# Values of all heads of a branch in one unit with 512 columns moving, and fewer filler steps inside the attention

## The chip, the cores and the metric

One core of a Trainium2 chip runs the program once per measurement. The metric is device time in microseconds (us), lower is better. Engines: PE (matmul), DVE, ACT, POOL, SP; PEld is PE's weight load.

## What is computed

One transformer block on x (512 tokens, width 1024), float32. The reference, cut to what matters:

```python
h = h + 0.5 * swiglu(rmsnorm(h, ffn1_norm), ffn1_w_gu, ffn1_w_down)
u = rmsnorm(h, mix_norm)
qa, ka, va, qb, kb, vb, qi, ki, wi, g = jnp.split(u @ w_in, SPLIT_POINTS, axis=-1)
# 8 heads of 64 in each branch; q and k are normalised per head
out_a = dsa_attention(qa, ka, va, qi, ki, wi, bias_dsa)  # keys: the top 256 by an index score
out_b = moba_attention(qb, kb, vb, bias_moba)            # keys: blocks of 256
g_a, g_b = jnp.split(sigmoid(g + b_gate), 2, axis=-1)
mixed = g_a * (out_a @ w_branch_dsa) + g_b * (out_b @ w_branch_moba)
h = h + mixed @ w_out
h = h + 0.5 * swiglu(rmsnorm(h, ffn2_norm), ffn2_w_gu, ffn2_w_down)
```

## The kernel before, in words

Activations lie transposed: a tile holds 128 features by 512 tokens. Every float32 factor is split into a high part (rounded to the fast matmul format) and the rest, and a product takes three matmuls, hi x hi, hi x lo and lo x hi (`mm3`, lines 125 to 128). Weights come through `wunit` (L119): one DMA of 128x1024 on SP's queue, one ACT copy to the high part (L111), POOL subtractions for the low part (L117); three buffers each.

The stages: first feed-forward layer (`ffn`; its `lead1` begins with four PSUM banks in turn, two `mm` and two `s`, three matmuls each), then q, k, values and index scores, the attention of branch 1 (moba), the mix of branch 1, the attention of branch 0 (dsa), the mix, the output projection and the second feed-forward layer.

PE's order is the program's own. The other engines' instructions are put in an order by a scheduler, which the program steers with priorities and, for the search of the top keys, with a table: `PIN` names after which of the 32 logits of branch 1's attention the search for query tile 1, 2 or 3 may begin. `topk` (L532) runs 16 rounds of MAX8, MATCH_VALUE_LOAD and MATCH_REPLACE8 on DVE for each tile; its result is added to the logits of branch 0 (L578).

`attention` (L551) is a generator that walks 32 steps, i = 4 * head + query tile. At each it issues the logits of step i + 2 (L595, L596; DVE adds bias and finds the extremes at L604, ACT takes the exponential at L75), the transposes of step i (L636; ACT L646 and DVE L647 split the result), at every fourth the values product of the head before (L657, L658), and in branch 1 at every second an index score (`extra`). Between these it yields 1: `weave` then takes one step of the filler, a chain of other units. Before, there are three such steps per i. A filler step of a q, k or gate unit is one `mm3` with 512 columns; a unit has eight. `AHEAD_B` (12) and `AHEAD_A` (16) steps run ahead of the attention. What is left of the filler runs behind it.

A q unit's norm (L416) follows 4 steps after its post, a k unit's (L450, L451) 11 steps after (`later`, `tick`).

`v_units` (L467) makes the values of four heads of a branch for all tokens. There the activations are stationary and the weights move: 256 columns, four token tiles of eight k each, two tiles to a bank; a step is two `mm3`. The posts (L475 on ACT, L476 on DVE) write high and low parts. It runs four times: once before branch 1's attention (in the `s` banks), twice in that attention's filler and once in that of branch 0, in the three `mm` banks.

## Time and profile before

| what | value |
|---|---|
| median of 3 runs | 1142.54 us (1142.5 to 1144.0) |
| the profiled execution's own time | 1144.06 us |
| its span | 1142.3 us |
| mean granted clock of PE | 0.999 |
| busy: PE, DVE, ACT, POOL | 1133.5, 644.0, 468.9, 547.8 us |

The profile is of one execution; times in it count from the span's start. Busy time is the union of an engine's instructions. Matmuls overlap in the records, so their pace is read from the distance of their starts, not from their durations. A granted clock of 1.00 is the upper of two levels (2.4 GHz), 0.5 the lower (1.2 GHz).

### The profile page before, as it was taken

Reading aid. Unit: us, or ns where it says so; the run is one execution under the profiler, and the core shown is the slowest. Engines: PE = TensorE matmul, PEld = TensorE weight load, DVE = VectorE, ACT = ScalarE, POOL = GpSimd, SP = SyncE. Lnnn points to the kernel's source line nnn. Section 1 sums busy time; section 2 is a strip of 40 time slices with the busy share of each in tenths; the row PEclk is TensorE's granted clock in tenths of the full one; section 3 lists DMA queues with packets and bytes.
Section 4 is the critical chain, followed back from the end, with each engine's and each line's share of the span. In section 5 each row is a group of like instructions: output and inputs, shape, how many; then the busy total and the mean of one; then the engine's idle time right before and its main releaser. Section 6 shows DMA issues by size and latency. Waiting matters only on the chain.

```text
span 1142.3 us, 14230 instructions
## 1 busy us (share of the span) xinstructions
PE 1133.5 (99%) x5364; PEld 948.2 (83%) x5364; DVE 644.0 (56%) x966; ACT 468.9 (41%) x765; POOL 547.8 (48%) x438
## 2 busy tenths in 40 slices
PE   9999999999999999999999999999999999999998
PEld 7778888888888888888889888888888888888887
DVE  5864155622556358699958785754663156613651
ACT  6322122322235468767238765443332123312321
POOL 3444444444445674664565542174444444444442
PEclk9999999999999999999999999999999999999999
DMA  7233222322223222321332321422233232322222
GB/s 236 86 112 107 93 92 96 107 92 92 97 80 105 86 105 85 102 75 47 102 129 86 105 79 47 137 94 93 96 108 92 92 100 102 93 92 95 104 79 92
DMA packets 39580, 111.73 MB, mean 98 GB/s; under 512 B 4534, under 2 KB 9048, under 8 KB 39512
## 3 DMA queue, kind: packets, MB, share of 16 engines
q1 hardware_dynamic: 39368, 110.80, 29.4%
q8 instruction: 42, 0.69, 0.2%
q14 instruction: 26, 0.21, 0.1%
q10 hardware_dynamic: 144, 0.02, 0.0%
HBM read 108.64 MB, written 2.17 MB: 97 GB/s over the span
## 4 chain that ended last, share of the span: by engine, by line
PE 90%; DVE 5%; ACT 2%; issue 1%; POOL 1%; DMA 0%; SPq 0%; POOLq 0%; DVEq 0%; ACTq 0%
PE mm L126 21%; PE mm L127 21%; PE mm L128 21%; PE s L126 7%; PE s L128 7%; PE s L127 7%; PE pt L636 1%; DVE l L604 1%; PE s L595 1%; PE s L596 1%; PE o L658 1%; PE o L657 1%; POOL wlo L117 1%; ACT tmp L75 1%; DVE work L541 0%
## 5 line engine op out<-in xcount | busy, mean ns | idle before, releaser
L117 POOL TENSOR_TENSOR wlo<-raw,whi 128x256 fp32r<-128x256 f32 (+2 forms) x344 | 490.4, 1444 | 532.2 <-ACT whi L111 526.2
L111 ACT ACTIVATE whi<-raw 128x1024 fp32r<-128x1024 f32 (+2 forms) x207 | 205.2, 993 | 527.2 <-PE mm L127 345.7
L126 PE MATMUL mm<-x,whi 128*128 128x512 f32 x632 | 251.5, 398 | 1.4 <-DVE v L476 1.1
L128 PE MATMUL mm<-x,wlo 128*128 128x512 f32 x632 | 246.6, 390 | 0.0
L127 PE MATMUL mm<-x,whi 128*128 128x512 f32 x632 | 246.6, 390 | 0.0
L127 PE MATMUL mm<-a,whi 128*128 128x512 f32 (+1 forms) x462 | 178.7, 387 | 0.3
L126 PE MATMUL mm<-a,whi 128*128 128x512 f32 (+1 forms) x462 | 178.5, 386 | 0.0
L128 PE MATMUL mm<-a,wlo 128*128 128x512 f32 (+1 forms) x462 | 178.5, 386 | 0.0
L128 PEld LDWEIGHTS mm<-x,wlo 128*128 128x128 f32 x632 | 118.6, 188 | 25.7 <-DVE wlo L113 0.4
L126 PEld LDWEIGHTS mm<-x,whi 128*128 128x128 f32 x632 | 118.9, 188 | 24.1 <-DVE v L476 1.5
L126 PE MATMUL s<-x,whi 128*128 128x512 f32 x352 | 137.0, 389 | 0.6 <-ACT tmp L75 0.6
L127 PE MATMUL s<-x,whi 128*128 128x512 f32 x352 | 136.9, 389 | 0.0
L128 PE MATMUL s<-x,wlo 128*128 128x512 f32 x352 | 136.9, 389 | 0.0
L127 PEld LDWEIGHTS mm<-x,whi 128*128 128x128 f32 x632 | 119.0, 188 | 21.2 <-issue 0.5
L279 DVE SCALAR_TENSOR_TENSOR h<-mm,h 128x512 f32<-128x512 f32 (+1 forms) x49 | 33.4, 681 | 166.6 <-PE mm L128 166.6
L270 DVE TENSOR_TENSOR tmp<-tmp,tmp 128x512 f32<-128x512 f32 x44 | 99.0, 2249 | 29.3 <-ACT tmp L75 29.1
L154 DVE TENSOR_TENSOR a<-tmp,a 128x512 fp32r<-128x512 f32 x49 | 89.5, 1828 | 28.5 <-ACT a L153 28.3
L127 PEld LDWEIGHTS mm<-a,whi 128*128 128x128 f32 x462 | 86.8, 188 | 18.6 <-DVE a L154 1.1
L126 PEld LDWEIGHTS mm<-a,whi 128*128 128x128 f32 x462 | 86.8, 188 | 17.7
L128 PEld LDWEIGHTS mm<-a,wlo 128*128 128x128 f32 x462 | 86.8, 188 | 17.6
L126 PEld LDWEIGHTS s<-x,whi 128*128 128x128 f32 x352 | 66.0, 187 | 14.7 <-ACT tmp L75 1.0
L127 PEld LDWEIGHTS s<-x,whi 128*128 128x128 f32 x352 | 66.1, 188 | 13.8
(172 smaller groups left out, 1338.3 us busy)
## 6 DMA issues: line engine op xcount, KB each, us to landing
raw<-in_ffn_w_gu_dram SPq DMA_DIRECT2D x84, 512.0 KB, 3.5
raw<-in_w_in_dram SPq DMA_DIRECT2D x35, 512.0 KB, 3.5
raw<-in_ffn_w_down_dram SPq DMA_DIRECT2D x32, 512.0 KB, 3.5
raw<-in_ffn_w_down_dram SPq DMA_DIRECT2D x16, 384.0 KB, 3.1
bias<-fd SPq DMA_DIRECT2D x16, 256.0 KB, 3.4
raw<-in_w_v_dram SPq DMA_DIRECT2D x8, 512.0 KB, 3.4
raw<-in_w_out_dram SPq DMA_DIRECT2D x8, 512.0 KB, 3.5
h<-in_x_dram SPq DMA_DIRECT2D x8, 256.0 KB, 4.3
```

The lines of the kernel that those rows point to most:

```text
L75: op = after([group["load"]], lambda: nc.scalar.activation(*a, **k))
L111: nc.scalar.activation(hi, raw, AF.Copy)
L117: eng.tensor_sub(lo[:, b], raw[:, b], f32(hi)[:, b])
L126: nc.tensor.matmul(pt, wh, xh, start=start, stop=False)
L127: nc.tensor.matmul(pt, wh, xl, start=False, stop=False)
L128: nc.tensor.matmul(pt, wl, xh, start=False, stop=stop)
L154: nc.vector.tensor_sub(lo, src, f32(hi))
L270: nc.vector.tensor_mul(g1, g1, s)
L279: nc.vector.scalar_tensor_tensor(h[c][:, b], pd, 0.5, h[c][:, b], op0=ALU.mult, op1=ALU.add)
L595: nc.tensor.matmul(p[:, 0:N], qb, k[:, e, 0:N], start=True, stop=False)
L596: nc.tensor.matmul(p[:, 0:N], qb, kl[:, e, 0:N], start=False, stop=True)
L604: sums[i] = nc.vector.tensor_tensor_reduce(out=pe, in0=p[:, 0:W], in1=pe, scale=f[:, 2 * qt + e:2 * qt + e + 1], scalar=3e38, op0=ALU.add, ...
```

## The change

A value unit now makes all eight heads of a branch: weights move with 512 columns, one PSUM bank per token tile, four banks open at once, a step is one `mm3`, 32 steps to a unit. The values of pair 0 lie in a `g` buffer, those of pairs 1 to 3 in one `v` buffer. The unit of branch 1 runs wholly before its attention, that of branch 0 between the two attentions, in front of branch 1's mix. The attention of branch 1 takes two filler steps per i instead of three, that of branch 0 two and three in turn. All searches for top keys begin behind the last logits of branch 1. Gate 0 stands before the last pair's units of branch 0, and gates 3 to 6 lie in `g` and `q` buffers two by two. The columns of `w_v` are laid out anew on the host (eight units of 256 rows by 512 columns).

```diff
--- before.py
+++ after.py
@@ -30,7 +30,7 @@
 TMPS, RAWS = 7, 3
 AHEAD_A, AHEAD_B, GATES, GATES_B = 16, 12, 7, 3
 
-PIN, EVERY = (0, 20, 28, 31), 2
+PIN, EVERY = (0, 31, 31, 31), 2
 
 LAG, LAG_Q = 11, 4
 
@@ -464,38 +464,31 @@
 
         later(LAG, norm)
 
-    def v_units(br, j, dsts, bank=mmps):
-
-
-        vs = []
-
-        def post(t, p):
-            for e, v in enumerate(vs):
-                src = p[:, e * P:(e + 1) * P].rearrange("p (e d) -> p e d", e=2)
-                nc.scalar.activation(v[:, t, :, 0, :], src, AF.Copy, scale=r2T[:, t:t + 1])
-                nc.vector.scalar_tensor_tensor(v[:, t, :, 1, :], src, r2T[:, t:t + 1], f32(v)[:, t, :, 0, :],
-                                               op0=ALU.mult, op1=ALU.subtract)
-
-        ws = [wunit(w_v[4 * br + 2 * j + i]) for i in range(2)]
-        wh, wl = ([a.rearrange("p k c -> p (k c)").rearrange("p (k c) -> p k c", k=4)[:, k] for a in w for k in range(4)]
-                  for w in zip(*ws))
-        for t in range(NQ):
-            if t % 2 == 0:
-                p = bank()
-            o = p[:, (t % 2) * 256:(t % 2 + 1) * 256]
-            b = slice(t * P, (t + 1) * P)
-            for k in range(KD):
-                mm3(o, us[k][0][:, b], us[k][1][:, b], wh[k], wl[k], k == 0, k == KD - 1)
-                if k % 2:
+    def v_units(br, heads, banks):
+
+
+        va, vb = T("g", 1, (P, 2, S), F32R), T("v", 1, (P, 6, S), F32R)
+        va, vb = (a.rearrange("p n c -> p (n c)").rearrange("p (t e s d) -> p t e s d", t=NQ, s=2, d=DH)
+                  for a in (va, vb))
+        for j, dst in enumerate(heads):
+            v = va if j == 0 else vb[:, :, 2 * j - 2:2 * j]
+            dst.append(v.rearrange("p t e s d -> p t e (s d)"))
+        for m in range(4):
+            wh, wl = (a.rearrange("p k c -> p (k c)").rearrange("p (k c) -> p k c", k=2) for a in wunit(w_v[4 * br + m]))
+            for t, p in enumerate(banks):
+                b = slice(t * P, (t + 1) * P)
+                for i in range(2):
+                    k = 2 * m + i
+                    mm3(p, us[k][0][:, b], us[k][1][:, b], wh[:, i], wl[:, i], k == 0, k == KD - 1)
                     tick()
                     yield
-            if t == 1:
-                vs.extend(T("v", 3, (P, NQ, 2, 2, DH), F32R) for _ in dsts)
-                for v, dst in zip(vs, dsts):
-                    dst.append(v.rearrange("p t e s d -> p t e (s d)"))
-            if t % 2:
-                post(t - 1, p[:, 0:256])
-                post(t, o)
+        for t, p in enumerate(banks):
+            src = p.rearrange("p (e d) -> p e d", d=DH)
+            r = r2T[:, t:t + 1]
+            for v, c in ((va, src[:, 0:2]), (vb, src[:, 2:8])):
+                nc.scalar.activation(v[:, t, :, 0, :], c, AF.Copy, scale=r)
+                nc.vector.scalar_tensor_tensor(v[:, t, :, 1, :], c, r, f32(v)[:, t, :, 0, :],
+                                               op0=ALU.mult, op1=ALU.subtract)
 
     def qk_units(br, pr, q, k):
         u = (U_QA, U_QB)[br] + pr
@@ -682,7 +675,8 @@
                 values(i // 4 - 1)
             if extra and i % EVERY == 0:
                 extra.pop(0)()
-            yield 1
+            if sel and i % 2:
+                yield 1
         yield 3
         values(7)
 
@@ -703,12 +697,10 @@
     def gate(gi, keep):
 
         def post(p):
-            if gi in (3, 4):
-                g1 = T("g", 2)
-            elif gi in (5, 6):
-                if gi == 5:
-                    wide.append(T("q", 2, (P, 2, S)))
-                g1 = wide[0][:, gi - 5, :]
+            if 3 <= gi <= 6:
+                if gi % 2:
+                    wide.append(T("g", 1, (P, 2, S)) if gi == 3 else T("q", 2, (P, 2, S)))
+                g1 = wide[-1][:, 1 - gi % 2, :]
             else:
                 g1 = tmp()
             nc.vector.tensor_mul(g1, p, r2)
@@ -729,14 +721,15 @@
     def qk(br, pr):
         return qk_units(br, pr, *(dsa, moba)[br][pr][0:2])
 
-    def vv(br, j, **kw):
-        return v_units(br, j, [a[2] for a in (dsa, moba)[br][2 * j:2 * j + 2]], **kw)
+    def vv(br, banks):
+        return v_units(br, [a[2] for a in (dsa, moba)[br]], banks)
 
     piece[0] = 256
     ps3 = [mmps() for _ in range(2)]
     together([mmk(p, wunit(w_in[U_QB + 4 * i]), us) for i, p in enumerate(ps3)])
-    v0 = vv(1, 0, bank=sps)
-    next(v0)
+    v0 = vv(1, [sps(), sps(), T("o", 1, p=ps), mmps()])
+    for _ in range(2):
+        next(v0)
     r2 = norm_r(ss2)
     for _ in range(6):
         next(v0)
@@ -762,19 +755,19 @@
     ob, oa = [], []
     extra = [lambda qt=qt, hd=hd: score(qt, hd) for qt in range(1, NQ) for hd in range(4)]
     gates = {}
-    fill = chain(qk(1, 1) + qk(1, 2) + [vv(1, 1)] + qk(1, 3) + [gate(KD + c, gates) for c in range(GATES_B)]
-                 + qk(0, 0) + [vv(0, 0)])
+    fill = chain(qk(1, 1) + qk(1, 2) + qk(1, 3) + [gate(KD + c, gates) for c in range(GATES_B)] + qk(0, 0))
     weave(attention(1, moba, ob, extra), fill, AHEAD_B)
     run(fill)
     for qt in range(1, NQ):
         topk(qt)
+    run(vv(0, [sps(), sps(), T("o", 1, p=ps), tps()]))
     mixb = [T("a", 16) for _ in range(KD)]
     for c in range(KD):
         if c + GATES_B < KD:
             run(gate(KD + c + GATES_B, gates))
         g1 = opened(KD + c)
         run(branch(wb_b, c, ob, lambda p: nc.vector.tensor_mul(mixb[c], p, g1)))
-    fill = chain(qk(0, 1) + qk(0, 2) + [vv(0, 1)] + qk(0, 3) + [gate(c, gates) for c in range(GATES)])
+    fill = chain(qk(0, 1) + qk(0, 2) + [gate(0, gates)] + qk(0, 3) + [gate(c, gates) for c in range(1, GATES)])
     weave(attention(0, dsa, oa, []), fill, AHEAD_A)
     run(fill)
     flush()
@@ -871,8 +864,7 @@
     add("ffn1_w_down", _units(w["ffn1_w_down"]))
     add("w_in", _units(w["w_in"], [c + P * i for c, n in ((C_QA, 4), (C_KA, 4), (C_QB, 4), (C_KB, 4), (C_QI, 2),
                                                           (C_KI, 1), (C_G, 16)) for i in range(n)]))
-    add("w_v", np.concatenate([_units(w["w_in"][r:r + S], [c], 256) for c0 in (C_VA, C_VB) for c in (c0, c0 + 256)
-                               for r in (0, S)]))
+    add("w_v", np.concatenate([_units(w["w_in"][r:r + 256], [c], 512) for c in (C_VA, C_VB) for r in range(0, D, 256)]))
     for name in ("w_branch_dsa", "w_branch_moba", "w_out", "ffn2_w_gu", "ffn2_w_down"):
         add(name, _units(w[name]))
     add("rel_bias", inputs["rel_bias"])
```

Three places show how instructions move. In PE's order, branch 1's attention, between the transposes of a third query tile (pt<-ident, four) and the next logits (s<-k). Before:

```order
L636 MATMUL pt_3699<-ident,l_3539 128x128 x4
L126 MATMUL mm_3686<-x_2422,whi_3688 128x512
L127 MATMUL mm_3686<-x_2423,whi_3688 128x512
L128 MATMUL mm_3686<-x_2422,wlo_3689 128x512
L126 MATMUL mm_3686<-x_2455,whi_3688 128x512
L127 MATMUL mm_3686<-x_2456,whi_3688 128x512
L128 MATMUL mm_3686<-x_2455,wlo_3689 128x512
L595 MATMUL s_3712<-k_3221,q_3172 128x384
```

and now:

```order
L629 MATMUL pt_3443<-ident,l_3322 128x128 x4
L126 MATMUL mm_3338<-x_2587,whi_3340 128x512
L127 MATMUL mm_3338<-x_2588,whi_3340 128x512
L128 MATMUL mm_3338<-x_2587,wlo_3341 128x512
L588 MATMUL s_3453<-k_3249,q_3192 128x384
```

One filler step of three matmuls instead of two stands between them.

In DVE's order, where the search begins (MAX; L604 and L597 are the same instruction of the logits). Before, behind the 24th logits (the table allows it from the 21st):

```order
L604 ISA l_4042,st_4067<-s_4062,l_4042,fq_3492 128x512
L604 ISA st_4067 128x1
L538 MAX m_4576<-work 128x8
L647 TENSOR_TENSOR pt_2640<-pt_4073,pt_2639 128x128
L541 MATCH_REPLACE work<-m_4576,work 128x256
L614 RECIPROCAL recip_2645<-tot_3797 128x8
L538 MAX m_4579<-work 128x8
L647 TENSOR_TENSOR pt_2640<-pt_4073,pt_2639 128x2x128
L541 MATCH_REPLACE work<-m_4579,work 128x256
```

and now, behind the 32nd, the last:

```order
L597 ISA l_4138,st_4164<-s_4161,l_4138,fq_3854 128x512
L597 ISA st_4164 128x1
L531 MAX m_4296<-work 128x8
L534 MATCH_REPLACE work<-m_4296,work 128x256
L531 MAX m_4299<-work 128x8
L640 TENSOR_TENSOR pt_2640<-pt_4170,pt_2639 128x128
L607 RECIPROCAL recip_2646<-tot_3974 128x8
L534 MATCH_REPLACE work<-m_4299,work 128x256
L640 TENSOR_TENSOR pt_2640<-pt_4170,pt_2639 128x2x128
L531 MAX m_4302<-work 128x8
L534 MATCH_REPLACE work<-m_4302,work 128x256
L657 TENSOR_TENSOR os_4190<-o_4181,tmp_4191 64x512
```

The splits of the last head's transposes (L640, before L647) and the sum of a head's values (L657) now stand among the first rounds of the search for tile 1, which before had begun two heads earlier.

In PE's order, a value unit. Before, in the filler of branch 1's attention:

```order
L126 MATMUL mm_3560<-whi_3395,x_2391 128x256
L127 MATMUL mm_3560<-wlo_3396,x_2391 128x256
L128 MATMUL mm_3560<-whi_3395,x_2392 128x256
L126 MATMUL mm_3560<-whi_3395,x_2422 128x256
L127 MATMUL mm_3560<-wlo_3396,x_2422 128x256
L128 MATMUL mm_3560<-whi_3395,x_2423 128x256
L595 MATMUL s_3630<-k_3221,q_3172 128x256
```

and now, behind that attention (s_4443 and s_4444 are the banks of two token tiles):

```order
L126 MATMUL s_4443<-whi_4450,x_2391 128x512
L127 MATMUL s_4443<-wlo_4451,x_2391 128x512
L128 MATMUL s_4443<-whi_4450,x_2392 128x512
L126 MATMUL s_4443<-whi_4450,x_2422 128x512
L127 MATMUL s_4443<-wlo_4451,x_2422 128x512
L128 MATMUL s_4443<-whi_4450,x_2423 128x512
L126 MATMUL s_4444<-whi_4450,x_2391 128x512
L127 MATMUL s_4444<-wlo_4451,x_2391 128x512
L128 MATMUL s_4444<-whi_4450,x_2392 128x512
L450 MATMUL mm_4467<-tmp_4233,bd 128x512
```

The second operand, which moves, has 512 columns instead of 256, a bank is left after two `mm3`, and no logits stand between.

## Rows read from the trace of the kernel before

**Rows 1.** The page, part 1: busy time, share of the span, instructions of each engine.
```profile
PE 1133.5 (99%) x5364; PEld 948.2 (83%) x5364; DVE 644.0 (56%) x966; ACT 468.9 (41%) x765; POOL 547.8 (48%) x438
```

**Rows 2.** Waits of PE: engine, line, releaser; total us, times, longest.
```profile
PE mm L126 <- DVE v L476: 1.1, 1, 1.1
PE s L595 <- DVE st L604: 0.8, 1, 0.8
PE pt L636 <- DVE pt L647: 0.6, 1, 0.6
PE pt L416 <- ACT tmp L405: 0.5, 1, 0.5
PE pt L748 <- ACT tmp L745: 0.3, 1, 0.3
PE pt L748 <- DVE R L235: 0.2, 1, 0.2
```

**Rows 3.** Windows: stretch, length, busy us (x instructions), granted clock, DMA share, GB/s.
```profile
200.00:300.00 100.00, 100.00 (x443) 82.81 (x442) 39.92 (x35) 26.47 (x30) 45.57 (x19) 1.00 0.30 99
```

**Rows 4.** Timeline of PE in a value unit: first and last of 16.
```profile
384.00 0.28 PE L128 MATMUL s<-whi,x 128*128 128x256 f32 x1
...
385.79 0.28 PE L128 MATMUL s<-whi,x 128*128 128x256 f32 x1
```

**Rows 5.** Groups by form, PE, matmuls of the value units.
```profile
L126 PE MATMUL mm<-whi,x 128*128 128x256 f32 x96 | 28.7, 299 | 0.0
L126 PE MATMUL s<-whi,x 128*128 128x256 f32 x32 | 9.6, 301 | 0.0
```

**Rows 6.** Windows, attention of branch 1: heads 0 to 5, head 1, head 6, head 7.
```profile
420.40:497.60 77.20, 76.45 (x453) 67.11 (x452) 57.62 (x143) 61.95 (x144) 48.47 (x66) 1.00 0.26 86
429.80:443.30 13.50, 12.75 (x71) 10.65 (x70) 11.88 (x28) 11.09 (x26) 7.91 (x11) 1.00 0.26 82
497.60:510.10 12.50, 12.50 (x67) 10.54 (x66) 12.20 (x40) 6.86 (x16) 7.66 (x12) 1.00 0.29 84
510.10:521.40 11.30, 11.30 (x61) 9.57 (x60) 10.63 (x34) 5.95 (x14) 6.89 (x9) 1.00 0.17 46
```

**Rows 7.** Groups by form, ACT and DVE, 420.4 to 497.6.
```profile
L111 ACT ACTIVATE whi<-raw 128x1024 fp32r<-128x1024 f32 x9 | 9.5, 1061 | 0.9 <-PE mm L127 0.4 <-POOL work L530 0.4
L475 ACT ACTIVATE v<-mm,r2T 128x128 fp32r<-128x128 f32 x8 | 3.0, 369 | 1.6 <-PE mm L128 1.5
L476 DVE SCALAR_TENSOR_TENSOR v<-mm,r2T,v 128x128 fp32r<-128x128 f32 x8 | 2.8, 346 | 1.3 <-ACT v L475 1.3
```

**Rows 8.** Windows, attention of branch 0: heads 0 to 6, then heads 1, 2, 5.
```profile
599.60:685.50 85.90, 84.80 (x493) 73.82 (x492) 67.67 (x164) 66.31 (x150) 44.94 (x54) 1.00 0.27 90
608.80:622.30 13.50, 13.50 (x90) 12.18 (x89) 12.28 (x28) 11.48 (x23) 11.15 (x12) 1.00 0.26 87
622.30:634.60 12.30, 12.30 (x98) 11.99 (x97) 10.74 (x30) 10.75 (x27) 2.23 (x3) 1.00 0.17 56
661.50:673.40 11.90, 11.90 (x64) 10.04 (x63) 11.22 (x25) 8.22 (x18) 8.30 (x10) 1.00 0.21 65
```

**Rows 9.** Groups by form, ACT and DVE, 599.6 to 685.5.
```profile
L475 ACT ACTIVATE v<-mm,r2T 128x128 fp32r<-128x128 f32 x8 | 2.7, 356 | 0.0
L476 DVE SCALAR_TENSOR_TENSOR v<-mm,r2T,v 128x128 fp32r<-128x128 f32 x8 | 2.6, 343 | 0.0
```

**Rows 10.** Windows, the end of branch 1's attention.
```profile
523.00:529.00 6.00, 4.85 (x36) 4.19 (x34) 5.80 (x17) 5.15 (x10) 2.81 (x4) 0.98 0.18 65
529.00:532.30 3.30, 3.30 (x18) 3.30 (x17) 3.24 (x8) 2.69 (x5) 0.00 (x0) 0.52 0.27 71
```

**Rows 11.** Search for the top keys, DVE: groups in 407 to 545, then line 538.
```profile
L538 DVE MAX8 m<-work 128x8 f32<-128x256 f32 x16 | 6.7, 421 | 0.2
L541 DVE MATCH_REPLACE8 work<-m,work 128x256 f32<-128x256 f32 x16 | 6.5, 409 | 0.0
L541 DVE MATCH_VALUE_LOAD work<-m,work 128x8 f32 x24 | 2.0, 84 | 0.4
L538 DVE MAX8 m<-work 128x8 f32<-128x384 f32 x9 | 5.0, 555 | 0.1
L541 DVE MATCH_REPLACE8 work<-m,work 128x384 f32<-128x384 f32 x8 | 4.3, 541 | 0.0
L538 DVE MAX8 m<-work x48: 377/561/696, 496.3 to 581.9; 128x8 f32<-128x256 f32 x16, 128x8 f32<-128x384 f32 x16, 128x8 f32<-128x512 f32 x16
```

**Rows 12.** Window in lead1 of the first feed-forward layer.
```profile
8.00:25.00 17.00, 17.00 (x76) 13.94 (x75) 12.60 (x21) 12.73 (x22) 4.42 (x3) 1.00 0.84 267
```

## The prediction

> **What bounds the kernel now.** I read the engines' totals first: PE is busy 1133.5 of 1142.3 us, no other engine above 58% [rows 1]. Next the waits of PE: nine, one of each kind, 5.5 us together; the four that this change can touch are 1.1 us on the value post (DVE v L476), 0.8 on the logits' evacuation (DVE st L604), 0.6 on a split of the transposed probabilities (DVE pt L647) and 0.5 on the squares of a query unit (ACT tmp L405) [rows 2]. So time falls only by PE needing less, by those waits, or by clock; it rises by new waits. Then windows by stage, for the share of ACT and DVE beside PE.
>
> **The pace of PE.** Over 100 us of the first feed-forward layer 443 matmuls with 512 columns start, 0.2257 us each [rows 3]. In a value unit, from 384.00 to 385.79, sixteen matmuls with 256 columns start, 1.79 / 15 = 0.1193 us each [rows 4]. Two narrow ones cost 0.2386, one wide one 0.2257. A filler step is three wide matmuls, 0.677 us; a value step of before is six narrow ones, 0.716.
>
> **Part 1: wide values.** 3 x (96 + 32) = 384 narrow matmuls [rows 5] take 45.8 us; 192 wide ones 43.3. PE is full there, so this is on the path: **-2.5**. The Trainium skill, page TensorE: Matmul & The Clock Gate, section on the 56 ns gap, gives a full-speed matmul N / 2.4 GHz plus about 2.5 ns; by it I estimate a gain of 0.5 us only (192 times 2.6 ns), and the sum below would be 2.0 us less. The rows' price is taken, since they time this kernel's own operands. The posts are 8 ACT and 8 DVE instructions a branch instead of 16 and 16, and lie beside PE's next units, which write other PSUM banks: nothing. Eight 512 KB loads stay eight loads on SP's queue, each now due 24 matmuls (5.4 us) after the last like any other unit's; before, both halves were due within 24 narrow ones. Nothing either. Gate 0 is moved ahead of the last pair's units of branch 0, and gates 3 and 4 share the buffer that held pair 0's values: written at filler step 80 and later, read last by the second head's values at step 44 or so. Nothing.
>
> **Part 2: the first value unit.** Two steps stand ahead of the norm's matmul instead of one, six behind it as before; those six are 0.04 us shorter each, and PE then waits for the norm (DVE R L235, ACT tmp L745 [rows 2]), so that wait grows by 6 x 0.04: **+0.2**.
>
> **Part 3: attention of branch 1 (B).** From its first logits to those of head 6 (420.4 to 497.6) PE is busy 76.45 of 77.2 us, ACT 61.95, DVE 57.62 [rows 6]. 22 iterations lose a step each: the 16 value steps and six more. PE loses 16 x 0.716 + 6 x 0.677 = 15.5, and needs 60.9. ACT loses the value copies (3.0) and three of the nine weight splits (3 x 1.06) [rows 7]: 55.8 left, a share of **0.915**. DVE loses 2.8 [rows 7] and the start of the search: about 54, 0.89. What share can ACT hold before PE waits? Three readings. Head 1 (429.8 to 443.3) has ACT at 11.09 / 13.5 = 0.82, and there PE waits 0.8 for L604 [rows 2, 6]. In branch 0 a head runs with ACT at 10.75 / 12.3 = 0.874 and none [rows 8]. DVE ran at 12.20 / 12.5 = 0.98 without a wait of PE [rows 6], so DVE is not the limit. At 0.874 the stretch takes 55.8 / 0.874 = 63.8, 2.9 over what PE needs; the 0.8 of before is inside this, so net **+2.1**. Bounds: -0.8 (ACT manages 0.915) and 55.8 / 0.82 = 68.0, that is +6.3. I take the middle row, since it is a whole head that ran clean; heads 6 and 7 have only gates as filler, with ACT under 0.55 [rows 6], and cost nothing.
>
> **Part 4: the end of B and the search for the top keys.** Before, the search may start at the 21st logits and starts at 496.3 [rows 11], and the filler at the end is a value unit with the norms of k and q among it. Between 523 and 529 DVE is busy 5.80 of 6.0 us, PE idles 1.15 (the 0.5 and the 0.6) and from 529.0 to 532.3 the granted clock is 0.52, the lower of the two levels: 18 matmuls in 3.3 us, which at 0.1193 take 2.1, so 1.2 lost [rows 2, 10]. Now the last two filler units are a k and a q unit whose norms come after the attention, and the search starts behind the last logits. I remove 2.3 and give 0.4 back, since some four rounds of the search (0.42 + 0.08 + 0.41 us each [rows 11]) now stand between the last splits that PE needs: **-1.9**; ends -2.3 and 0. The pins set only the order on DVE, so nothing queues behind a wait of theirs. The search itself: 48 rounds, some 15 us at 256 columns, 19 at 384 (0.56 + 0.08 + 0.54) and 23 at 512 (the 0.70 of the longest maximum, as much for its replacement) [rows 11], 57 us on DVE, with some 20 of posts among them. From the last logits of B to the first of A PE has the rest of the attention (nine steps, two heads' values, some 9 us), six filler steps (4), the values (21.7), 72 steps of the mix (49) and 16 steps ahead (11): 95 us against 77. Covered; were it not, A's first addends would be late by the difference. The 32 value steps that leave B and the 16 that leave A run where PE has no waits now: PE time moved, not added.
>
> **Part 5: attention of branch 0 (A).** Seven heads take 85.9 us, PE busy 84.8; the 1.1 missing is the wait on DVE v L476, a value post that held one of three mm buffers [rows 2, 8]. That post is gone: **-1.1**. 14 steps leave these heads (16 value steps out, two others in), so PE needs 84.8 - 11.5 + 1.4 = 74.7. ACT loses 2.7 and two splits: 61.5, 0.82. DVE loses 2.6: 65.1, 0.87 [rows 8, 9]. Heads at 12.28 / 13.5 and 11.22 / 11.9 of DVE ran clean [rows 8]. Ends -1.1 and +2 (two heads with a wait of B's kind and size).
>
> **Sum.** -2.5 + 0.2 + 2.1 - 1.9 - 1.1 = -3.2. The profiled execution took 1144.06 us (span 1142.3), so its like would be 1140.9; the median of the runs, 1142.54, lies 1.5 lower, which puts the forecast at **1139.3**. Measurement tells about 0.2%, 2.3 us, from no change.
>
> **The rivals.**
> - *ACT becomes the bound of B (slower).* Its exponentials, k copies and weight splits stand in one fixed order, and each exponential waits for DVE's L604 just ahead. If ACT holds no more than the 0.82 of head 1, B costs 6.3, and an idle PE can fall to the lower clock as it did at 529, so I count no gain at the end nor in A: -2.5 + 0.2 + 6.3 = +4.0, **1146.5**. It decides from a share of about 0.84 down. For it: the one wait of B's heads came at 0.82, and five steps instead of seven now lie between a head's logits and their transposes. Against it: the clean head at 0.874.
> - *The gains come back as other waits (same).* The search meets the last heads' splits as before, and some other post holds an mm buffer in A: parts 4 and 5 give nothing, -2.5 + 0.2 + 2.1 = -0.2, **1142.3**. For it: DVE is again without a pause behind the last logits.
> - *The value unit that turns through four banks loses the clock.* Every six matmuls it changes bank. If PE idled a little at each change and the clock fell, the two stretches of 21.7 us would take twice as long, **+43**, 1182. Against it: lead1 turns through four banks every three matmuls between 8 and 25 us with clock 1.00 and PE busy 17.00 of 17.00 [rows 12]. The Trainium skill, page TensorE: Matmul & The Clock Gate, section A second HAM failure mode, says that cycling through PSUM banks each iteration made the clock swing; rows 12 do not bear it out here.
>
> **How the numbers follow.** Forecast 0.50, ACT-bound B 0.25, gains come back 0.23, clock lost 0.02. The low end is all bounds in my favour: -2.5 - 0.8 - 2.3 - 1.1 = -6.7, 1135.8. The high end is the slower rival's price, 1146.5, which leaves out half of that rival, the clock case and a little below: about 0.18. Faster by over 0.2%: 0.45 of the forecast's 0.50 and 0.02 of the third case, 0.47. Slower: 0.23 and 0.02, with 0.01 of others, 0.26. The rest, 0.27, is within 0.2%.
>
> **What would show it.** Right: value matmuls 0.226 us apart in two stretches without waits, of some 21.7 us each, at clock 1.00; no PE wait on a value post; B from first logits to head 6 in 62 to 65 us with ACT near 0.87; no stretch at the lower clock; the search ended before A's first logits. Wrong: PE waits in B on L604, on exponentials or on k copies that add up to over 5 us, clock below 1 there, or PE waiting on topk's results at A's start.

## The result, and the profile after

The changed kernel takes **1154.57 us** (median; 1153.81 to 1155.42), beside 1143.27 for the kernel before on the same chip: ratio 1.0097 [1.0082, 1.0112]. It is slower by 11.3 us, where the forecast of 1139.3 had it 3.2 less. Executions of the kernel before lie near 1142.6 us at a mean granted clock of 1.000 or near 1144.1, mostly at 0.999; the one profiled, 1144.06, is of the second kind. The changed kernel's profiled execution took 1155.42 us, its span is 1153.3. Lines after the value units stand 7 lower than before: L588 and L589 are the logits (L595, L596), L597 their evacuation (L604), L629 the transposes (L636), L639 and L640 the split of the transposed probabilities on ACT and DVE (L646, L647), L607 the reciprocal of the sums.

The page of the changed kernel, part 1, answers to [rows 1]:

```profile
PE 1135.8 (98%) x5172; PEld 938.9 (81%) x5172; DVE 646.1 (56%) x950; ACT 465.9 (40%) x749; POOL 544.1 (47%) x438
```

PE has 192 matmuls fewer, as meant, and DVE and ACT 16 instructions fewer each. Yet PE's busy time is up by 2.3 us: some of it ran at the lower clock. Its waits (engine, line, releaser; total us, times, longest), beside [rows 2]:

```profile
PE pt L629 <- DVE pt L640: 6.0, 6, 2.4
PE pt L629 <- DVE fq L419: 2.7, 2, 2.5
...
PE pt L608 <- DVE recip L607: 0.8, 2, 0.5
PE mm L126 <- ACT whi L111: 0.7, 1, 0.7
...
PE o L650 <- ACT pt L639: 0.5, 1, 0.5
PE s L588 <- DVE st L597: 0.5, 1, 0.5
PE pt L741 <- DVE R L235: 0.4, 1, 0.4
```

The wait on the value post (L476) and the two at the end of branch 1 are gone. In their place PE waits to transpose, because the two banks that take the transposes (tile pt) come back late from DVE. Windows of the same kernel (columns as in [rows 3]): the second value unit; branch 1 from its first logits to those of head 6, its head 3 (heads count from 0), the low clock in it; branch 0 from its first logits to those of head 7, its head 1.

```profile
532.90:555.50 22.60, 22.60 (x105) 18.77 (x104) 21.47 (x59) 14.38 (x22) 11.64 (x16) 1.00 0.18 66
431.20:501.40 70.20, 64.49 (x338) 53.07 (x338) 54.71 (x128) 57.30 (x132) 39.90 (x53) 0.98 0.22 72
461.70:476.90 15.20, 12.55 (x64) 10.58 (x63) 13.67 (x27) 12.34 (x29) 6.66 (x7) 0.89 0.17 50
469.30:472.70 3.40, 3.40 (x10) 2.77 (x10) 2.81 (x6) 3.35 (x8) 0.59 (x1) 0.54 0.35 77
615.30:698.80 83.50, 78.75 (x406) 66.42 (x406) 67.51 (x157) 61.98 (x140) 37.65 (x49) 0.96 0.24 80
623.80:638.50 14.70, 12.34 (x58) 10.14 (x58) 11.60 (x26) 10.34 (x22) 8.60 (x12) 0.88 0.17 54
```

The value unit is clean. Branch 1's stretch takes 70.2 us (62 to 65 forecast), branch 0's 83.5 (74.7 needed). Three single gaps of PE stand out, longer than its usual spacing by 2.64 us (from 465.7), 2.53 (626.4) and 2.55 (653.2), and from 3.0 to 3.5 us after the start of each the granted clock is at its lower level for 3.4 us (from 469.0, 629.4, 656.7). In the first of these stretches matmuls with 512 columns start 0.43 us apart, not 0.226, which loses 1.6 us. In this execution each long wait thus costs some 4.2 us, and the three 12.5.

For all kernels below I use one measure, the **excess**: for each matmul the time to the start of the next, less the usual spacing of its shape, summed over a stretch. The usual spacing is the median in the kernel before: 0.227 us for 512 columns, 0.175 for 384, 0.120 for 256, 0.108 for 128 and 0.112 for 2. It holds waits and low clock alike. The expectations below count such losses in an earlier way that gives up to some 2 us more in a stretch. The medians come from several chips, on which the kernel before took 1142.7 to 1144.0.

| kernel | median us | excess, branch 1 (420 to 540) | excess, branch 0 (580 to 740) |
|---|---|---|---|
| before | 1143.3 | 5.4 | 2.6 |
| after | 1154.6 | 11.5 | 9.5 |
| hurry | 1154.4 | 16.7 | 3.8 |
| hurry2 | 1148.6 | 10.5 | 3.9 |
| nolow | 1150.2 | 9.2 | 7.3 |
| nolow_h | 1143.1 | 7.1 | 1.7 |
| p128h | 1144.9 | 9.1 | 3.1 |
| pad | 1170.9 | 2.5 (to 560) | 1.5 |
| spread7 | 1157.2 | 14.5 | 8.4 |
| lightB | 1151.3 | 8.6 | 8.7 |
| pin | 1156.0 | 12.4 | 7.9 |
| b_pin | 1142.4 | 2.0 | 4.1 |
| late18 | 1141.4 | 4.8 | 3.2 |

From before to after the excess grows by 13.0 us in the two attentions, while PE's work falls by some 2: that is the result.

What DVE does in a long wait, in the timeline of the changed kernel (start, length, engine, line; waits in brackets):

```profile
624.67 3.01 POOL L117 TENSOR_TENSOR wlo<-raw,whi 128x256 fp32r<-128x256 f32 x4 [5.59 <-ACT whi L111]
624.95 0.71 DVE L424 SCALAR_TENSOR_TENSOR fq<-fq 128x8 f32<-128x8 f32 x1
624.97 0.49 ACT L639 ACTIVATE pt<-pt 128x384 fp32r<-128x384 f32 x1
...
625.78 0.57 DVE L425 SCALAR_TENSOR_TENSOR fq<-fq,r2q 128x8 f32<-128x8 f32 x1
...
626.16 0.40 PE L128 MATMUL mm<-x,wlo 128*128 128x512 f32 x1
626.27 0.68 DVE L441 TENSOR_TENSOR tmp<-mm,R 128x512 f32<-128x512 f32 x1
...
627.27 0.96 DVE L461 SCALAR_TENSOR_TENSOR low<-tmp,gqk,k 64x512 fp32r<-64x512 f32 x1
...
628.27 0.49 DVE L640 TENSOR_TENSOR pt<-pt,pt 128x384 fp32r<-128x384 f32 x1
...
628.92 0.52 PE L629 MATMUL pt<-ident,l 128*128 128x128 f32 x3 [2.36 <-DVE pt L640]
```

ACT finished its half of the split at 625.46. DVE takes the other half 2.8 us later: the query norm (L424, L425), a key post (L441), an evacuation and a key's low part (L461) go first, and eight columns take 0.71 and 0.57 us while POOL works. Two theories follow: the order of DVE's queue, and DVE's pace beside POOL. A third lies behind both: the value steps that left were spacing for key and query posts.

### The profile page after: what moved, and what is told of

It reads as the page before. It is cut to its first block, busy times and chain, and to the rows that moved or that the text cites. A ratio compares the mean times of both kernels' runs of the same rounds, so it can differ in the third digit from the quotient of the medians.

```text
span 1153.3 us, 13825 instructions
## 1 busy us (share of the span) xinstructions
PE 1135.8 (98%) x5172; PEld 938.9 (81%) x5172; DVE 646.1 (56%) x950; ACT 465.9 (40%) x749; POOL 544.1 (47%) x438
## 4 chain that ended last, share of the span: by engine, by line
PE 92%; DVE 4%; ACT 2%; issue 1%; POOL 1%; DMA 0%; SPq 0%; DVEq 0%; ACTq 0%; POOLq 0%
PE mm L126 21%; PE mm L128 21%; PE mm L127 21%; PE s L126 8%; PE s L128 7%; PE s L127 7%; PE pt L629 1%; PE s L588 1%; PE s L589 1%; DVE l L597 1%; PE o L651 1%; PE o L650 1%; PE pt L416 0%; ACT tmp L75 0%; DVE pt L640 0%
## 5 line engine op out<-in xcount | busy, mean ns | idle before, releaser
L126 PEld LDWEIGHTS s<-x,whi 128*128 128x128 f32 x352 | 66.1, 188 | 14.7 <-ACT tmp L75 1.0
```

Of the source, the lines that this page charges most:

```text
L126: nc.tensor.matmul(pt, wh, xh, start=start, stop=False)
```

## The experiments

**Order on DVE.** `hurry` and `hurry2` change only priorities:

```
+                with tc.high_priority(HURRY):
                     nc.scalar.activation(dst(pth), src, AF.Copy)
                     nc.vector.tensor_sub(dst(ptl), src, dst(f32(pth)))
   hurry2 also:
+            with tc.high_priority(HURRY):
                 nc.vector.reciprocal(r1[:, 0:8], tot.pop(pr))
```

> The split of the transposed probabilities (ACT L639, DVE L640) gets the same priority in the engines' order as the exponentials; nothing else changes. Theory 1 (slack): PE waits because a pt bank comes back late, the split standing behind longer work in DVE's fixed order, with two filler steps fewer to cover that. Then the 8.7 us that PE's transposes wait on L640 and L419 fall under 3, at most one of the three stretches at the lower clock is left, and the time falls by about 8, to 1146 to 1148. Theory 2 (load): with fewer steps per head ACT and DVE have more work than PE gives them time for, in whatever order. Then the waits turn up at other places (logits, weights, values) and the time stays within 2 of 1154.6.

> The changed kernel with high priority for the two halves of the probabilities' split and for the reciprocal of the sums, so that DVE and ACT take them ahead of key and query posts. Order theory (PE waits because DVE takes work that nobody waits for first): with both kinds hurried the waits of over 1 us go, 1145 to 1149 us. Load theory (DVE and ACT are locally full): what is pushed back is a post or an addend that PE needs a little later, the waits change place once more, 1152 to 1157 us.

`hurry`: 1154.41 us, 1.0096 [1.0081, 1.0111], no different from the change. The waits on the split are nearly gone, and the next in the queue took their place. Waits of PE, then windows around the longest, in that kernel:

```profile
PE pt L608 <- DVE recip L607: 6.3, 4, 2.7
PE s L588 <- DVE st L597: 1.2, 3, 0.5
...
PE pt L629 <- DVE pt L641: 0.7, 1, 0.7
```

```profile
474.00:477.40 3.40, 0.69 (x4) 0.54 (x4) 3.33 (x7) 2.39 (x6) 2.11 (x3) 0.97 0.16 60
477.40:484.20 6.80, 6.17 (x20) 4.79 (x19) 3.20 (x9) 2.47 (x8) 2.69 (x6) 0.51 0.11 39
```

PE waits for a reciprocal of eight columns while DVE is busy 3.33 of 3.40 us, and the clock stays low for 6.8. Branch 0's excess fell from 9.5 to 3.8, branch 1's grew from 11.5 to 16.7. With the reciprocal hurried too (`hurry2`), 1148.61 us, 1.0044 [1.0030, 1.0058]: 6 us of the loss are order. Waits of up to 1.3 us stay there, on L597.

**Spacing.** `y3a` gave branch 0 its third filler step per iteration back, with no further units; `spread7` put gates between the pairs and began 24 steps ahead; `pad` put idle matmul steps where the value steps had been:

```
y3a:
-            if sel and i % 2:
+            if sel:
spread7 (branch 1, and so in branch 0 with gates 0 and 1):
-    fill = chain(qk(1, 1) + qk(1, 2) + qk(1, 3) + [gate(KD + c, gates) for c in range(GATES_B)] + qk(0, 0))
+    fill = chain(qk(1, 1) + [gate(KD, gates)] + qk(1, 2) + [gate(KD + 1, gates)] + qk(1, 3)
+                 + [gate(KD + c, gates) for c in range(2, GATES_B)] + qk(0, 0))
pad (branch 1; in branch 0 one such pair stands behind qk(0, 2), and gate 0 goes back to the other gates):
+    fill = chain(qk(1, 1) + qk(1, 2) + [pad(8), pad(8)] + qk(1, 3)
+                 + [gate(KD + c, gates) for c in range(GATES_B)] + qk(0, 0) + [pad(8), pad(8)])
-            if sel and i % 2:
-                yield 1
+            yield 1
```

> Branch 0's attention takes three filler steps per i again, as before the change; the 104 steps of its filler then run out 14 steps early. If the count of steps sets the waits, the two waits of 2.4 us in heads 1 and 3 of that attention and the two stretches at the lower clock after them go (8.4 us together), and the last heads wait about 2 to 4 us more for want of filler: 1149 to 1151. If the waits come from something else (the values' new place, the moved gate), they stay and the time rises to 1156 or more.

1157.86 us, 1.0127 [1.0112, 1.0142]: worse by 3.3. The long wait of head 1 went (its excess falls from 4.3 to 0.9), head 3 still lost 3.6, and the last head, where the filler had run dry, 5.2.

> The changed kernel with gate units between the key and query units of the pairs in both attentions (pair 1, a gate, pair 2, a gate, pair 3, the other gates) and a longer start (24 steps ahead in both) so that the last pair still comes in time. Density theory: the posts are further apart, fewer or shorter waits, 1145 to 1151 us. If it is the total load of the attentions and not its spacing, or if the gates' results held earlier leave too few of the seven working buffers: 1153 to 1158 us.

1157.15 us, 1.0112 [1.0095, 1.0128], a miss. From its first logits (440.6) the first five heads lose 2.2 us of excess, where the changed kernel's lose 8.2, so spacing, with the longer start, did help those heads. Then PE waited 3.1 us on k copies (L460), which I put down to the working buffers that the gates hold, without having tried it, and where the filler ran out 4.3 us on the split (L639).

> The changed kernel with three filler steps an iteration again, and with sixteen steps of matmuls that nobody reads, and that have no post, in each attention, just where the value units stood before (between the units of pairs 2 and 3, and behind the fill of branch 1 and behind pair 2 in branch 0). The 32 idle steps cost 32 x 0.677 = 21.7 us of PE. Density theory (the value steps were light padding between the key and query units, whose posts now come too close together for DVE and ACT): the PE waits of over 1 us in both attentions vanish, no low clock in them, heads take 12 to 14.5 us as before, and the time is about 1154.4 + 21.7 - 12 = 1164 us. Rival (the waits come from something else that the change moved: pair 0 and the other heads' values in new buffers, gate 0's place, the pin): waits of 2.5 us stay, 1172 to 1176 us.

1170.85 us, 1.0242 [1.0228, 1.0256]. The expectation priced 32 idle steps, but the kernel it describes has 48, with those behind branch 1's fill: 48 x 0.677 = 32.5 us, so that the density theory should have said 1174.9 and the rival 1183 or more. Windows over both attentions:

```profile
420.00:560.00 140.00, 139.25 (x710) 117.47 (x710) 99.21 (x250) 91.67 (x196) 75.81 (x101) 1.00 0.22 72
620.00:740.00 120.00, 120.00 (x618) 101.11 (x617) 81.29 (x186) 79.92 (x173) 50.88 (x61) 1.00 0.23 75
```

One wait of 0.8 us is left, and no low clock. Values in their new buffers and the pins are in this kernel, so they do not make the waits by themselves: PE time without posts between the units takes the waits away. Gate 0 stands in its old place here, so this run says nothing of its move; `late18` below has the gate in its new place and no long wait in branch 0. Whether the idle steps help by spacing or by lowering the average load, this run can't say; `spread7`'s first heads speak for spacing.

`lightB` and `light` tried useful padding: the index key and query units in branch 1's filler (scores from iteration 8, in another order), then gates among branch 0's pairs; `light_h` adds the hurry.

> The changed kernel with work that has light posts put into branch 1's attention in the place of the value steps: the index key and the two index query units (24 steps), which stood before the attention, now lie between the key and query units of the pairs, with three filler steps an iteration; the scores start at iteration 8. PE's work is the same. Density theory: branch 1's stretch (420 to 540) loses some 5 us instead of 13, as in the run with idle steps and before; branch 0 stays as it is: 1145 to 1148 us. If useful steps with posts of their own are no padding: 1153 to 1157 us.

> As the run before it in branch 1, and in branch 0 gates 0, 3 and 4 between the units of the pairs, 22 steps ahead. Density theory: both attentions lose some 5 us, no wait over 1.5 us, 1138 to 1143 us, the level of the kernel before or a little under it. Rival: branch 0 gains nothing, since gates held early take working buffers: no better than the run before it.

> As the run before it, with the high priority of the second hurried run (split of the probabilities, reciprocal). If what is left are waits by order on DVE, 2 to 4 us less than the run before it, 1136 to 1140 us and under the kernel before; else the same as that run.

1151.34 us (1.0077 [1.0063, 1.0091]), 1153.32 (1.0095 [1.0081, 1.0108]) and 1149.14 (1.0061 [1.0049, 1.0074]). Branch 1 gained 2.9 of the 8 hoped for, branch 0 nothing in `light` (10.1): all three miss their first theory, and steps with posts of their own are poor padding. Only the gain of the hurry, 4.2 us, came as hoped, or a little over.

**POOL beside DVE.** `nolow` lets the filler's units use the high part of the weights three times; `nolow_h` adds hurry2; `p128h` is hurry2 with POOL's pieces half as long. The first two leave out the weights' low part and so can't be kept:

```
nolow:  +            return (hi.rearrange("p (k c) -> p k c", c=P),) * 2
p128h:  -    piece[0] = 256      +    piece[0] = 128
```

> The changed kernel with the low parts of the filler units' weights left out in both attentions: each of these units multiplies by the high part three times, so PE, ACT, the loads and the posts are as they were, but POOL makes no subtraction of 128x1024 for them (19 units a run, some 5 us of POOL each). It leaves out part of the projections' precision. Contention theory (DVE is full there because its instructions take longer while POOL works): DVE's 128x8 steps fall from some 0.6 us to 0.16 and the splits and evacuations with them, PE's waits of 2.5 us and the low clock go, 1143 to 1147 us. Rival (the number of posts alone fills DVE and ACT): DVE's durations or at least PE's waits stay, 1152 to 1156 us.

> The hurried kernel (split of the probabilities and reciprocal at high priority) with the low parts of the filler units' weights left out as in the run without POOL's subtractions. Alone the first took 5.9 us off the changed kernel and the second 4.4. If they mend different causes (what DVE takes first; how long its instructions take beside POOL): both add up, 1143 to 1146 us, no wait of PE over 1.2 us. If they mend the same waits: 1147 to 1149 us.

> The hurried kernel with POOL's subtractions for the weights in pieces of 128 columns and not 256, so that a DVE instruction that is held by a POOL instruction is held for half as long. If the length of POOL's single instruction sets the delay: DVE's 128x8 steps beside POOL fall from 0.55 to some 0.35 us and the time to 1145 to 1147 us. If what counts is POOL's busy time in all (more instructions, more of it): 1148 to 1151 us.

1150.17 us, 1.0062 [1.0046, 1.0077]; 1143.07, 1.0002 [0.9993, 1.0012]; 1144.86, 1.0015 [1.0006, 1.0024]. In `nolow` 24 units (not 19) make no subtraction, and POOL's busy time falls from 544.1 to 471.7 us. Its time lies between the two theories; its longest wait of PE is still on the split:

```profile
PE pt L634 <- DVE pt L645: 5.1, 3, 2.9
```

`nolow_h`, without any wait over 1.2 us, says why: alone the hurry takes off 5.9 us and the missing subtractions 4.4, together 11.5. They mend different things, and together they give back the loss. Single lines on DVE from 420 to 720 (shortest/median/longest ns, first and last start), of the changed kernel:

```profile
L423 DVE TENSOR_TENSOR fq<-fq x7: 149/158/577, 444.1 to 676.8; 128x8 f32<-128x8 f32 x7
L424 DVE SCALAR_TENSOR_TENSOR fq<-fq x7: 148/550/721, 445.8 to 679.9; 128x8 f32<-128x8 f32 x7
L454 DVE TENSOR_TENSOR tmp<-tmp,tmp x7: 678/690/1358, 445.2 to 676.2; 128x512 f32<-128x512 f32 x7
```

and the same three steps in `nolow`, whose lines stand 5 higher:

```profile
L428 DVE TENSOR_TENSOR fq<-fq x7: 153/159/164, 445.5 to 671.6; 128x8 f32<-128x8 f32 x7
L429 DVE SCALAR_TENSOR_TENSOR fq<-fq x7: 155/159/659, 446.0 to 672.5; 128x8 f32<-128x8 f32 x7
L459 DVE TENSOR_TENSOR tmp<-tmp,tmp x7: 677/683/700, 444.4 to 671.9; 128x512 f32<-128x512 f32 x7
```

The longest of L423 falls from 577 to 164 ns, of L454 from 1358 to 700. L454 in `hurry2` and in `p128h`, which differ in POOL's pieces alone:

```profile
L454 DVE TENSOR_TENSOR tmp<-tmp,tmp x7: 680/753/1245, 445.8 to 670.4; 128x512 f32<-128x512 f32 x7
L454 DVE TENSOR_TENSOR tmp<-tmp,tmp x7: 684/766/972, 445.1 to 667.3; 128x512 f32<-128x512 f32 x7
```

POOL's subtractions fall from 740 to 464 ns (medians), and eight-column steps (L423 to L425) beside them from at most 720 to at most 450 ns: a shorter POOL instruction holds DVE for less time. Beside POOL's longer L446 eight columns still take up to 1.26 us. The median of L424 alone would mislead: it is 166 ns in `hurry2`, where fewer of the seven meet POOL, and 319 in `p128h`.

**The pins (part 4).** `pin` puts the old pins, (0, 20, 28, 31), into the changed kernel, `b_pin` the new ones, (0, 31, 31, 31), into the kernel before.

> Only the table of the search is put back: the searches may begin at logits 20, 28 and 31 again. Theory: the late start saved the waits and the lower clock at the end of branch 1's attention that the kernel before had (2.3 us), and nothing else hangs on it; going back costs 1 to 3 us, 1156 to 1157.5. Rival: the search only shifts work that DVE has room for; no change, 1154.6 within 1.

> The kernel before with only the search for the top keys pinned behind the last logits of branch 1 (the change's table of pins, nothing else). Part 4 of the prediction by itself: the waits of 0.6 and 0.5 us at 525 to 528 and the low clock behind them go, 1.9 us less, about 1142.1 us, ratio 0.998. If the search meets the last splits all the same: 1144 us, no change. If the search starts too late for branch 0's first addends: slower, PE waits on the search at 599.

1156.0 us, 1.0110 [1.0095, 1.0125], and 1142.35, 0.9994 [0.9985, 1.0003]. The new pins are worth 1.4 us on the one kernel and 0.4 on the other, and neither can be told from nothing by its interval. Waits of PE in `b_pin`:

```profile
PE s L595 <- DVE st L604: 1.0, 2, 0.8
PE pt L416 <- DVE st L604: 0.7, 1, 0.7
```

The waits and the low clock at the end of branch 1 are gone; the second stretch of [rows 10] is now

```profile
529.00:532.30 3.30, 3.30 (x27) 3.21 (x26) 3.30 (x14) 3.26 (x7) 0.00 (x0) 1.00 0.17 50
```

A wait of 0.7 us for L416 has come, up to 617.5, in branch 0. The search there starts its last round at 595.5, not 581.9 [rows 11].

`pin` shows one thing more. Its profiled execution (1154.81 us) has the three long waits of the changed kernel again, 2.65, 2.52 and 2.55 us, but the low clock behind the last alone. Windows behind each:

```profile
468.40:473.00 4.60, 4.58 (x24) 3.96 (x25) 4.54 (x9) 4.51 (x10) 0.73 (x1) 1.00 0.17 57
629.80:634.00 4.20, 4.16 (x21) 3.59 (x22) 4.14 (x6) 1.98 (x4) 2.69 (x2) 1.00 0.29 112
655.40:658.80 3.40, 3.40 (x12) 2.82 (x10) 2.42 (x4) 2.55 (x5) 0.74 (x2) 0.50 0.00 0
```

So a wait of 2.5 us is not always followed by the lower clock. And with two such stretches fewer this execution is only 0.6 us shorter than the changed kernel's: where PE ran on at full clock, a wait of 1.3 us for a reciprocal came at 476.4, and the earlier search cost 1.0 more at the end of branch 1. In both executions the waits are the larger part of the loss, the clock the smaller.

**Banks.** `pv` moves the query norm's sums from the transposes' banks to the units': `pv = mmps()[:, 0:2 * NQ]`.

> The sums of squares of a q unit (L416) go to an mm bank instead of one of the two pt banks. Theory 1 says that the wait of 2.5 us on L419 in branch 1's attention is a pt bank held for a tiny result that DVE reads late: it goes, with the stretch at the lower clock behind it, about 4 us, 1150 to 1151; the waits on L640 in branch 0 stay. Rival: the transposes would have waited for L640 just behind L419 all the same: under 1 us of change.

1160.66 us, 1.0160 [1.0142, 1.0178]: worse by 6, with 6.5 us of waits for a unit's bank held by the query post. No bank is spare.

**What can be kept.** `b_pin_h` and `b_p128` put pins and hurry, then also the shorter pieces, on the kernel before.

> The kernel before with the change's pins and the high priority for split and reciprocal: what of the change and of the runs could be kept without moving the values. Its excess over PE's need is 12.7 us before and 11.0 with the pins; some 2.5 of it are waits on posts in the attentions. If hurrying helps only where DVE is full: 1142 to 1143, no change. If it helps here as well: 1140 to 1141, better than both kernels.

> As the run before it, with POOL's pieces at 128 columns. Same reasoning as for the pieces above, where there is less to win: 1139.5 to 1142.5 us if shorter pieces help DVE; over 1143 if more POOL instructions cost.

1144.21 us, 1.0013 [1.0004, 1.0022], and 1150.29, 1.0063 [1.0050, 1.0076]: both misses. In the first the wait on the value post grew to 1.9 us; in the second PE waited once, 3.7 us, for the index weights (L378), ahead of the attentions, with 6.8 us of low clock behind it. In the two attentions `b_p128` loses 8.2 us of excess and `b_pin_h` 9.5, so its time does not speak against the shorter pieces there.

`late8` and `late18` take `p128h` and move the twelve index scores of branch 1 to later iterations: `if extra and i > 7 and i % EVERY == 0:` and `if extra and i > 18:`.

> The hurried kernel with POOL's pieces of 128 columns, and the twelve index scores of branch 1's attention at iterations 8 to 30 and not 0 to 22, so that DVE and ACT have less to do in the heads that hold the key and query units (the kernel without this lost 8 us in branch 1 in waits before and behind scores, at 473 to 475 and 499). 1141 to 1144 us, waits of PE at scores under 1 us; if the scores' place is indifferent: 1144 to 1146.

> As the run before it with the scores at iterations 19 to 30, one in each, all in the heads that have gates as filler (heads 6 and 7 lost nothing so far). 1139 to 1142.5 us if these heads take them, at or under the kernel before; if one score an iteration holds both banks of the logits there, the waits move to 500 to 518 and it is 1144 us or more.

`late8`: 1146.13 us, 1.0025 [1.0016, 1.0034], no help. `late18`: **1141.40 us, 0.9986 [0.9977, 0.9994]**, a little under the kernel before. Its longest waits of PE:

```profile
PE o L172 <- DVE tmp L169: 1.1, 1, 1.1
PE s L588 <- ACT tmp L515: 0.9, 1, 0.9
PE pt L609 <- DVE recip L608: 0.9, 1, 0.9
PE s L588 <- ACT k L460: 0.7, 1, 0.7
```

None is long, and its clock is never low in the attentions. So some 1.5 us of the forecast 3.2 is there once three loads are taken off the same heads: the order on DVE, POOL's long pieces, and the scores. Late scores were not tried on the kernel before.

## Why the prediction was wrong

**Part 1 (-2.5) held.** Wide value matmuls in the changed kernel's timeline:

```profile
540.19 0.39 PE L126 MATMUL s<-whi,x 128*128 128x512 f32 x1
...
543.59 0.39 PE L126 MATMUL pt<-whi,x 128*128 128x512 f32 x1
```

Fifteen starts in 3.40 us, 0.2267 each: 192 take 43.5 us, 2.3 less than 384 narrow ones. By the Trainium skill (TensorE: Matmul & The Clock Gate, the section on the 56 ns gap) I estimate a start every 0.2158 us and a gain of 0.5; these starts don't fit that, and the measurement decides. The value unit turned through four banks at clock 1.00.

**Part 2 (+0.2) held:** the wait on R grew from 0.2 to 0.4.

**Part 3 (+2.1) failed, and it is the main step.** The stretch cost 9.3 over PE's 60.9. I took a share of ACT, 0.874, "a whole head that ran clean", as what the kernel can hold, and set DVE aside because of "12.20 / 12.5 = 0.98 without a wait of PE". Both readings fail. And the sum gave the low clock no term in this stretch, where the profiled execution had 3.4 us of it. That 0.98 stood in head 6, where the search ran in DVE's gaps; nobody in the attention waits for the search, so a full DVE there shows nothing of what it can hold of work that PE waits for. And a head's mean hides the 5 us that decide. Windows in the changed kernel around the three long waits:

```profile
463.00:468.40 5.40, 2.75 (x16) 2.13 (x17) 4.95 (x10) 4.04 (x10) 2.35 (x2) 1.00 0.02 8
624.00:629.00 5.00, 2.64 (x15) 1.93 (x14) 4.93 (x13) 4.35 (x10) 3.57 (x6) 1.00 0.08 11
650.50:656.00 5.50, 3.11 (x18) 2.35 (x18) 5.00 (x14) 2.83 (x8) 1.47 (x2) 1.00 0.40 143
```

DVE is busy 4.93 of 5.00 us at 624, in a head whose mean is 11.60 / 14.7 = 0.79, well under the 0.91 and 0.94 of the heads of branch 0 that I called clean [rows 8]. The waits come from what stands ahead of one split in DVE's queue. The mean hides it for a second reason: the wait itself has lengthened the head. Against what PE needs of these heads (length less excess, 10.6 us in branch 1's head 3 and 10.4 in branch 0's head 1) DVE has 13.67 and 11.60 us of work, 1.29 and 1.12 times as much; in the kernel before the highest of these heads is at 1.00. I had spread DVE's work evenly over six heads (0.89), and it does not lie evenly.

**Part 4 (-1.9) was too large:** the stalls at 523 to 532 went, but by the medians it is 0.4 us on the kernel before and 1.4 on the one after. Trace against trace `b_pin` loses 3.4 us less in branch 1 and 1.5 more in branch 0, where the wait for L416 is, and its span is 1.7 us shorter (1140.6, 1142.3). The 1.7 is against the profiled execution of the kernel before, with its low clock at 529; the median lay 1.5 lower already. The sum took off both this 1.5 and part 4's 1.2 for the clock, which are largely the same loss.

**Part 5 (-1.1) failed the same way.** The post that held a bank did go. Its upper end of +2 took "two heads with a wait of B's kind and size"; two waits of 2.5 came, each with some 1.6 us lost to the lower clock behind it, and the excess there grew by 6.9.

**The rivals.** "ACT becomes the bound of B" had the place and the sign, and the clock behind it; its engine was wrong (DVE releases the two long kinds of wait, [rows 2] against the list above), and it put nothing in branch 0, where half the loss is. It said 1146.5; 1154.6 came. The rival that lets the gains come back as other waits had waits in both attentions, but no loss beyond part 3's 2.1; it fell by its size. The four-bank rival fell.

Not separated: how much of the loss is spacing and how much the higher average load, and why a wait of some 2.5 us is answered by 3.4 us of low clock, in `hurry` by 6.8 and in `pin` twice by none.

## What to carry to other kernels

A filler step is PE time and also the room that other engines' posts need: before light steps are taken out of a woven stretch, look at what each engine's queue holds in the few microseconds ahead of the instruction that PE waits for, not at shares over a head that holds the wait itself. A full engine shows capacity only if what fills it is work that somebody waits for. And a wait of PE can cost more than its length: three waits of 2.5 us cost some 4.2 each where the lower clock followed, while `pin` had two of them without it.

## What the runs showed that I had not expected

In the changed kernel DVE steps of eight columns with two tiles in SBUF as input (L423 to L425) took 0.30 to 0.72 us where a POOL instruction lay beside them and 0.15 to 0.17 where none did. One turn, in branch 1's head 3 (L453, L454 and POOL's L660 read two SBUF tiles each):

```profile
464.93 0.69 DVE L453 SCALAR_TENSOR_TENSOR tmp<-tmp,tmp 128x512 f32<-128x512 f32 x1
464.98 1.77 POOL L660 TENSOR_TENSOR os<-os,rb 128x512 f32<-128x512 f32 x1 [0.31 <-DVE os L657]
465.94 1.36 DVE L454 TENSOR_TENSOR tmp<-tmp,tmp 128x512 f32<-128x512 f32 x1
```

L453 came first and kept its 0.69 us; POOL, which came second, took 1.77; L454 came while POOL was at work and took 1.36, not 0.69. This is part of the first long wait; in the third (653.2) POOL is idle until 654.5, and order alone makes the wait. The split L640, which reads PSUM and one tile in SBUF, keeps its length (median 460 ns in the changed kernel, 479 in `nolow`). The Trainium skill, page SBUF — State Buffer, section SBUF: two separate sides, says that a DVE instruction with two SBUF inputs and a GpSimd one take a shared port in turn, each for its whole length; the rows above agree, as does the shorter hold with shorter pieces.

A single wait of 2.5 us in a dense stretch can be followed by 3.4 us at 1.2 GHz: three of three in the changed kernel, beginning 0.5 to 1.0 us after PE's return to work, but one of three in `pin` and one of two (2.53 and 2.56 us) in `lightB`.
